# A two-layer sequence kernel: the second layer's weights split once and kept in DRAM, or split again for each block

## The chip, the cores and the metric

The kernel runs on one core of a Trainium2 chip. The core has five engines that run side by side, each through its own list of instructions in order: TensorE (PE in the rows; PEld is its weight load), VectorE (DVE), ScalarE (ACT), GpSimd (POOL) and SyncE (SP), which here issues nearly all DMA transfers. They wait for each other through semaphores. The metric is the time of one execution in microseconds on the device, the median of three runs. A second source is one profiled execution, in which the start and the length of every instruction are recorded.

## What is computed

A trunk of two layers over a sequence of 2048 positions with 1024 channels, all in float32. The part of the reference that matters here:

```python
c_act = jax.nn.silu(c)
for i in range(DEPTH):                      # DEPTH = 2
    shift, scale, gate = jnp.split(c_act @ ada_w[i] + ada_b[i], 3, axis=-1)
    h = rms_norm(x, norm_pre[i]) * (1.0 + scale[:, None, :]) + shift[:, None, :]
    if i % 2 == 0:
        p = h @ ev_w_in[j]                  # 1024 x 4224
        ...                                 # a recurrence (RWKV-7) and a gated short convolution
        y = jnp.concatenate([y_a, y_b], axis=-1) @ ev_w_out[j]
    else:
        p = h @ od_w_in[j]                  # 1024 x 3080
        ...                                 # a 31-tap convolution with LayerNorm (C), a chunked state-space scan (D)
        y = jnp.concatenate([y_c, y_d], axis=-1) @ od_w_out[j]
    x = x + gate[:, None, :] * rms_norm(y, norm_post[i])
```

The input projection `h @ od_w_in` of the second layer is the place of the change.

## The kernel before

Products run in the float32r type. To keep float32 accuracy, each operand is split into two float32r parts: `hi` is a rounded copy (made by ScalarE, `CAST w<-x`), `lo` is what is left, `raw - hi` (made by GpSimd, `TENSOR_TENSOR w<-x,w`). Three products (hi hi, hi lo, lo hi) stand for one. A weight tile is 128 output channels wide: 1024 x 128 numbers, 512 KB as it lies in DRAM (tile `x`, 128 x 1024), 1 MB when split (two tiles `w` of 128 x 2 x 512). One job is one weight tile times one block of 512 positions: 8 contraction steps with three products each, 24 products of 128 x 512 into one PSUM bank `pp`.

Layer 0 goes over two halves of the sequence with 33 weight tiles each; each tile serves two blocks. Between its products stand the steps of the recurrence (tiles `ch`, `yp`, `UV`, `S`, `SC`, `X`, `BK`). Then comes its output projection, `out_proj`. Layer 1 goes over four blocks of 512 positions; for each block all 25 weight tiles are fetched and split again, so 100 jobs. Its side work is the 31-tap convolution (`conv31`: tile `co`, 24 taps a channel group on VectorE, five on ScalarE and GpSimd through `pr` and `cs`), the scan (`ssd_chunk`: `rep`, `xd`, `xw`, `sy`, `S`), the LayerNorm (`conf_out`) and the modulated rows of the next block (`hblock`: `h`, `act`). The last output projection ends the kernel.

The class `Feed` hands out weight tiles: `fetch` loads a raw tile into `x` (ring of two), `prepare` splits it into two `w` tiles (ring `wp` of four, so two jobs). In `run_jobs`, at the start of job n, the tile of job n+1 is split and that of job n+2 fetched. The transfers of the weights, of `rep`, of the rows `h` and of the results `y` all stand in SP's one list.

Work that is not a product is written as generators in queues (`bg`, `quick`, `ev`, `aux`, `post`, `tail`, `urgent`, `slow`). A product loop calls `tick` after every second product (layer 0) or every fourth (layer 1); a tick lets the first generator of each queue take a step. In layer 0 a step is held back until a small model of the engines' load (`Clock`) allows it. `slow` holds the modulation of both layers (loads of `ada_w` into `h`) and the gate row; it is emptied before `out_proj`. The framework then puts the instructions of each engine into their final order, which can move an instruction ahead of others that were written before it.

Of the kernel before, what the change touches and what calls it, by code (L numbers as in the profile page):

```python
# [9 lines left out]
F32 = mybir.dt.float32  # L10
# [8 lines left out]
P = 128  # L19
# [51 lines left out]
class Clock:  # L71
    """Estimate of when each engine gets through what has been issued to it, by which work is spread over the products."""
# [49 lines left out]
class Feed:  # L122
    """Weight tiles of a list of jobs: fetched two jobs ahead, split one job ahead."""
# [5 lines left out]
    def fetch(self):  # L129
        if self.jobs and len(self.raw) < 2:  # L130
            self.raw.append((self.jobs[0], self.trunk.raw(self.jobs.pop(0).src)))

    def prepare(self):
        if self.raw and len(self.w) < 2:
            job, r = self.raw.pop(0)
            self.w[job] = (job.split or self.trunk.split_w)(r)


class Trunk:
    def __init__(self, ctx, tc, I, out, T, dbg=None):  # L140
# [12 lines left out]
        self.wp = pool("wp", 4)  # L153
# [62 lines left out]
    def take(self, name, shape, bufs=1, busy=None):  # L216
        """A tile of a ring, once the last steps on the one that it follows are issued; free() ends its use."""
        ring = self.rings.setdefault((id(self.t) if name != "tr" else 0, name), [])
        while len(ring) >= bufs and id(ring[-bufs]) in self.inuse:
            yield busy  # L220
        t = self.tr.tile(shape, F32, name=name) if name == "tr" else self.t.tile(shape, F32, name=name, bufs=bufs)
        ring.append(t)
        self.inuse.add(id(t))
        return t
# [24 lines left out]
    def setup(self):  # L249
# [43 lines left out]
        self.y = [[self.dram.tile([P, KT, BL], F32, name=f"y{l}_{b}") for b in range(NBLK)] for l in range(2)]  # L293
        self.x1 = [self.dram.tile([P, D], F32, name=f"x1_{t}") for t in range(self.T // P)]

# [48 lines left out]
    def split_w(self, r, pool=None, bufs=4):  # L344
        w = []
        for z in range(2):
            t = (pool or self.wp).tile([P, 2, BL], F32R, name="w", bufs=bufs)
            self.split(t[:, 0], t[:, 1], r[:, z * BL:(z + 1) * BL])
            w.append(t)
        return lambda i, k: w[k // 4][:, i, (k % 4) * P:(k % 4 + 1) * P]  # L350

# [100 lines left out]
    def hblock(self, l, blocks, spread=1, places=None):  # L452
        """Modulated rows of blocks, in halves; those of the next half are fetched and normalized ahead where there is a place for them."""
# [57 lines left out]
    def first_blocks(self, begun):  # L511
        """Blocks 0 and 1 of layer 0, and the first projections, whose products follow each part of the modulated rows."""
# [79 lines left out]
        for d in range(KT):  # L592
            while raws and raws[0][0] < d:
# [3 lines left out]
                         (lambda w: [w[:, 0], w[:, 1]])(self.wp.tile([P, 2, BL], F32R, name="w")) for _ in range(2)]  # L597
# [576 lines left out]
    def odd(self, b):  # L1174
        W = lambda ti: self.I["w_in1"][ti]
        st = {"B": [None] * 2, "C": [None] * 2, "sz": [None] * 4, "co": [None] * 4, "cg": [None] * 4}
        jobs = [Job(W(24), lambda bl, ps: self.evac_dt(b, st, ps), mm=self.mm_dt, split=self.split_dt)]
# [150 lines left out]
    def split_dt(self, r):  # L1328
        nc = self.nc
        w = self.wp.tile([P, 2, BL], F32R, name="w")  # L1330
# [174 lines left out]
def tile_trunk(ctx, tc, I, out, T):  # L1505
# [4 lines left out]
    with ExitStack() as e:  # L1510
# [6 lines left out]
        k.slow += [k.modulation(0, range(16, 24), 1), k.modulation(1, range(24), 1), k.gate_row(0)]  # L1517
        halves = lambda name: tuple(k.t.tile([P, BL], F32, name=name, bufs=2) for _ in range(2))
# [83 lines left out]
```

## Time and profile before

| what | value |
|---|---|
| median of 3 runs | 2700.67 us (2700.13 to 2702.35) |
| profiled execution, first to last instruction | 2697.7 us |
| TensorE busy | 2418.6 us, 90% |
| VectorE busy | 1867.9 us, 69% |
| GpSimd busy | 1169.7 us, 43% |
| ScalarE busy | 1018.5 us, 38% |
| moved by DMA | 218.31 MB |

Busy time is the time in which an engine has an instruction running. It says nothing of what it waits for: a VectorE instruction that is slowed by something else counts as busy for all of its length. The profiled execution divides into layer 0's projections and recurrence (to about 1480 us), its output projection (to about 1600 us), layer 1's blocks (to about 2580 us) and the last output projection. The shares differ by stage, so they are read by stage below.

### The profile page before, as it was taken

How to read it: one execution, taken by the hardware profiler on the slowest of the kernel's cores; microseconds unless marked ns; L12 is line 12 of the kernel's file. 1: busy time of each engine (PE TensorE's matmuls, PEld its weight loads, DVE VectorE, ACT ScalarE, POOL GpSimd, SP SyncE). 2: the span in 40 equal slices, each digit the busy share in tenths (PEclk: the TensorE clock that was granted, in tenths of full speed). 3: DMA queues.
4: the chain of work that ended last, by engine and by line, in shares of the span. 5: the costliest groups of instructions: out<-in, count | busy, mean ns of one | idle time of the engine just before them, and what ended most of it. 6: DMA issues, size and time to landing. Idle time of an engine off the chain costs nothing.

```text
span 2697.7 us, 35944 instructions
## 1 busy us (share of the span) xinstructions
PE 2418.6 (90%) x13408; PEld 1828.1 (68%) x13408; DVE 1867.9 (69%) x3223; ACT 1018.5 (38%) x2058; POOL 1169.7 (43%) x1274
## 2 busy tenths in 40 slices
PE   5998999999999999999999989877888788688898
PEld 3675666766757667676776877765766676576687
DVE  5897664945768466584653126699899989999821
ACT  5423322233452332323332246434644544344231
POOL 5423223232242232423224544556566556656654
PEclk9998988989899998999999999898998899798999
DMA  6352110101211011010132433222322232222343
GB/s 237 101 174 73 44 32 29 40 29 48 71 37 40 32 37 36 32 47 24 44 107 86 154 139 118 98 71 75 105 87 67 102 102 86 86 98 67 110 147 126
DMA packets 101570, 218.31 MB, mean 81 GB/s; under 512 B 7442, under 2 KB 49682, under 8 KB 101396
## 3 DMA queue, kind: packets, MB, share of 16 engines
q1 hardware_dynamic: 101252, 215.76, 23.7%
q8 instruction: 105, 1.72, 0.3%
q14 instruction: 69, 0.57, 0.1%
q10 hardware_dynamic: 144, 0.26, 0.0%
HBM read 182.37 MB, written 33.62 MB: 80 GB/s over the span
## 4 chain that ended last, share of the span: by engine, by line
PE 45%; DVE 41%; POOL 4%; issue 4%; ACT 4%; DMA 2%; SPq 0%; DVEq 0%; POOLq 0%; ACTq 0%
PE pp L111 30%; DVE co L111 12%; PE tr L111 6%; PE yp L111 5%; PE ch L111 4%; DVE pr L111 3%; DVE X L111 3%; DVE BK L111 3%; DVE rep L111 2%; DVE sx L111 1%; POOL ss L111 1%; DVE act L111 1%; DVE sy L111 1%; DVE SC L111 1%; DVE sc L111 1%
## 5 line engine op out<-in xcount | busy, mean ns | idle before, releaser
L111 PE MATMUL pp<-act,w 128*128 128x512 f32 x7000 | 1878.4, 416 | 29.1 <-DVE yo L111 13.7
L111 PEld LDWEIGHTS pp<-act,w 128*128 128x128 f32 x7000 | 1325.0, 197 | 332.5 <-DVE yo L111 15.2
L111 POOL TENSOR_TENSOR w<-x,w 128x512 fp32r<-128x512 f32 x386 | 560.7, 1458 | 548.5 <-ACT w L111 544.6
L111 DVE SCALAR_TENSOR_TENSOR co<-u,cfw,co 128x512 f32<-128x512 f32 x384 | 388.7, 1028 | 4.8 <-ACT co L111 3.5
L111 ACT CAST w<-x 128x512 fp32r<-128x512 f32 x390 | 238.6, 619 | 234.3 <-PE pp L111 181.4
L111 POOL TENSOR_SCALAR sp<-S,PL 128x64 f32<-128x64 f32 x128 | 70.4, 552 | 278.0 <-DVE S L111 273.8
L111 ACT ACTIVATE UV<-ch,scal 64x64 f32<-64x64 f32 x256 | 79.3, 310 | 246.2 <-PE ch L111 242.5
L111 POOL TENSOR_TENSOR cs<-pr,cs 128x512 f32<-128x512 f32 x80 | 126.7, 1584 | 27.1 <-ACT cs L111 17.1
L111 DVE SCALAR_TENSOR_TENSOR S<-ch,PL,sp 128x64 f32<-128x64 f32 x128 | 36.0, 282 | 146.6 <-PE ch L111 141.6
L111 ACT ACTIVATE tA<-pp 128x512 f32<-128x512 f32 x96 | 57.2, 596 | 212.5 <-PE pp L111 140.3
L111 DVE TENSOR_TENSOR ss<-ss 128x1 f32<-128x1 f32 x60 | 12.6, 211 | 167.6 <-ACT tA L111 167.5
L111 DVE COPY z<-ch 128x64 f32<-128x64 f32 x128 | 28.6, 223 | 129.2 <-PE ch L111 126.4
L111 DVE TENSOR_TENSOR pr<-X,BK 128x2 f32<-128x2 f32 (+30 forms) x248 | 112.1, 452 | 6.5
L111 POOL COPY carry<-q 128x1 f32<-128x1 f32 (+1 forms) x84 | 21.5, 256 | 195.2 <-ACT q L111 119.3
L111 DVE TENSOR_TENSOR act<-yo,act 128x256 fp32r<-128x256 f32 (+1 forms) x104 | 52.7, 531 | 64.3 <-ACT act L111 63.7
L111 POOL COPY q<-carry 128x1 f32<-128x1 f32 (+1 forms) x84 | 29.9, 356 | 143.6 <-DVE tG L111 70.1
L111 DVE TENSOR_REDUCE X<-pr 128x1 f32<-128x2 f32 (+30 forms) x248 | 86.6, 349 | 6.6
L111 POOL TENSOR_SCALAR ss<-ss 128x1 f32<-128x1 f32 x80 | 30.6, 383 | 134.1 <-DVE ss L111 105.4
L111 PE MATMUL yp<-UV,SC 128*64 128x64 f32 x512 | 84.1, 250 | 0.0
L111 POOL TENSOR_TENSOR x<-x,yo 128x512 f32<-128x512 f32 x62 | 81.2, 1330 | 5.5 <-DVE yo L111 5.5
L111 PE MATMUL yp<-S,AR 64*64 64x64 f32 x512 | 78.0, 248 | 0.0
L111 ACT ACTIVATE pr<-u,cfw 128x512 f32<-128x512 f32 x80 | 56.2, 718 | 40.3 <-POOL cs L111 40.3
(288 smaller groups left out, 3385.5 us busy)
## 6 DMA issues: line engine op xcount, KB each, us to landing
x<-in_w_in_dram SPq DMA_DIRECT2D x163, 512.0 KB, 3.5
h<-in_ada_w_dram SPq DMA_DIRECT2D x32, 512.0 KB, 3.5
x<-y SPq DMA_DIRECT2D x32, 512.0 KB, 4.2
x<-x SPq DMA_DIRECT2D x32, 512.0 KB, 3.2
y<-yo SPq DMA_DIRECT2D x32, 256.0 KB, 2.2
h<-in_w_out_dram SPq DMA_DIRECT2D x16, 512.0 KB, 4.1
x<-in_x_dram SPq DMA_DIRECT2D x16, 512.0 KB, 3.5
rep<-acs SPq DMA_DIRECT2D x16, 512.0 KB, 4.8
```

The source lines that it names most:

```text
L111: return f(*args, **kw)
```

## The change

Layer 1's 24 full weight tiles are split once, during layer 0, by a new generator `presplit` at the end of the queue `slow`. For each half tile it loads 256 KB into `psr`, splits it into `psw` (one buffer each), and stores the 512 KB of `psw` to a DRAM tile `w1_j_z`. In layer 1, `Feed.fetch` calls `parts`, which loads the two stored parts into two `w` tiles; `prepare` only hands them on. The ring `wp` has six tiles in place of four, so three jobs. The 25th tile (the one for dt, `split_dt`) and the tiles of the output projections are split as before. The scratch memory for software DMA is set to 1024 bytes. Some comments and doc strings are removed; they do nothing.

```diff
     def fetch(self):
         if self.jobs and len(self.raw) < 2:
-            self.raw.append((self.jobs[0], self.trunk.raw(self.jobs.pop(0).src)))
+            job = self.jobs.pop(0)
+            self.raw.append((job, self.trunk.parts(job.src) if isinstance(job.src, list) else self.trunk.raw(job.src)))
     def prepare(self):
         if self.raw and len(self.w) < 2:
             job, r = self.raw.pop(0)
-            self.w[job] = (job.split or self.trunk.split_w)(r)
+            self.w[job] = r if isinstance(job.src, list) else (job.split or self.trunk.split_w)(r)
...
-        self.wp = pool("wp", 4)
+        self.wp = pool("wp", 6)
...
+        self.w1 = [[self.dram.tile([P, 2, BL], F32, name=f"w1_{j}_{z}") for z in range(2)] for j in range(24)]
...
+    def parts(self, src):
+        w = []
+        for z in range(2):
+            t = self.w_tile()
+            self.nc.sync.dma_start(out=t.bitcast(F32), in_=src[z])
+            w.append(t)
+        return self.picked(w)
+
+    def presplit(self, tiles):
+        for src, parts in tiles:
+            for z in range(2):
+                r = self.st.tile([P, BL], F32, name="psr", bufs=1)
+                self.nc.sync.dma_start(out=r.rearrange("p (k t) -> p k t", k=4) if len(src.shape) == 3 else r,
+                                       in_=src[:, z * BL:(z + 1) * BL])
+                yield True
+                yield
+                w = self.st.tile([P, 2, BL], F32R, name="psw", bufs=1)
+                self.split(w[:, 0], w[:, 1], r)
+                yield
+                self.nc.sync.dma_start(out=parts[z], in_=w.bitcast(F32))
+                yield
...
-        W = lambda ti: self.I["w_in1"][ti]
+        W = lambda ti: self.w1[ti]
-        jobs = [Job(W(24), lambda bl, ps: self.evac_dt(b, st, ps), mm=self.mm_dt, split=self.split_dt)]
+        jobs = [Job(self.I["w_in1"][24], lambda bl, ps: self.evac_dt(b, st, ps), mm=self.mm_dt, split=self.split_dt)]
...
         k.slow += [k.modulation(0, range(16, 24), 1), k.modulation(1, range(24), 1), k.gate_row(0)]
+        k.slow.append(k.presplit([(I["w_in1"][j], k.w1[j]) for j in range(24)]))
...
-    nc = bacc.Bacc("TRN2", target_bir_lowering=False, num_devices=1)
+    nc = bacc.Bacc("TRN2", target_bir_lowering=False, num_devices=1, dynamic_dma_scratch_size=1024)
```

Three places show what this does to the order. First SP's list early in layer 0, behind the second load of `w2a2`; before it reads:

```order
L111 DMA w2a_1584<-in_w2a_dram 128x128
L111 DMA x<-in_w_in_dram 128x1024
L111 DMA h<-in_ada_w_dram 128x1024 x3
L111 DMA x<-in_w_in_dram 128x1024
L111 DMA h<-in_ada_w_dram 128x1024 x4
L111 DMA x<-in_w_in_dram 128x1024
```

and now, with `w_0_0_117` the DRAM tile of weight tile 0, half 0:

```order
L111 DMA w2a_1632<-in_w2a_dram 128x128
L111 DMA psr<-in_w_in_dram 128x512
L111 DMA x<-in_w_in_dram 128x1024
L111 DMA w_0_0_117<-psw 128x1024
L111 DMA psr<-in_w_in_dram 128x512
L111 DMA x<-in_w_in_dram 128x1024
L111 DMA h<-in_ada_w_dram 128x1024 x2
L111 DMA w_0_1_118<-psw 128x1024
L111 DMA h<-in_ada_w_dram 128x1024
L111 DMA x<-in_w_in_dram 128x1024
```

The loads and stores of the half tiles stand between the weight loads of layer 0 and the loads for the modulation; 48 pairs follow each other like this, the last store ahead of the fifth `y<-sc` store.

Second, GpSimd's list in layer 1, where the third block's scan steps (`ss`) and convolution (`cs`, `ccf`) alternate; before:

```order
L111 TENSOR_TENSOR w<-x,w 128x512 x3
L111 COPY ccf<-u 128x30
L111 TENSOR_TENSOR cs<-pr,cs 128x512 x3
L111 TENSOR_TENSOR w<-x,w 128x512
L111 TENSOR_TENSOR cs<-pr,cs 128x512
L111 TENSOR_TENSOR w<-x,w 128x512
L111 TENSOR_TENSOR cs<-pr,cs 128x512
L111 TENSOR_TENSOR w<-x,w 128x512
L111 TENSOR_SCALAR ss<-ss 128x1
L111 TENSOR_TENSOR ss<-ss,nhalf 128x1
```

and now:

```order
L111 TENSOR_TENSOR ss<-ss,nhalf 128x1
L111 COPY ccf<-u 128x30
L111 TENSOR_TENSOR cs<-pr,cs 128x512 x5
L111 TENSOR_SCALAR ss<-ss 128x1
L111 TENSOR_TENSOR ss<-ss,nhalf 128x1
L111 COPY ccf<-u 128x30
L111 COPY u<-ccf 128x30
L111 TENSOR_TENSOR cs<-pr,cs 128x512 x5
```

The subtractions of the weight split are gone from between the other steps; nothing takes their place.

Third, SP's list at the start of layer 1's third block, around the loads of `rep`; before:

```order
L111 DMA x<-in_w_in_dram 128x1024 x6
L111 DMA acs_15587<-at 32x128
L111 DMA rep<-acs_15587 128x1024 x2
L111 DMA x<-in_w_in_dram 128x1024 x2
L111 DMA h<-x_10_127 128x1024
L111 DMA h<-x_11_128 128x1024
L111 DMA x<-in_w_in_dram 128x1024 x2
```

and now, with `w_12_0_141` the stored part of tile 12, half 0:

```order
L111 DMA w<-w_23_1_164 128x1024
L111 DMA acs_15813<-at 32x128
L111 DMA w<-w_12_0_141 128x1024
L111 DMA rep<-acs_15813 128x1024 x2
L111 DMA w<-w_12_1_142 128x1024
L111 DMA w<-w_13_0_143 128x1024
L111 DMA w<-w_13_1_144 128x1024
L111 DMA w<-w_14_0_145 128x1024
L111 DMA w<-w_14_1_146 128x1024
L111 DMA h<-x_10_175 128x1024
L111 DMA h<-x_11_176 128x1024
```

Two loads `w` stand where one load `x` stood. Each now waits for TensorE to have read the tiles that are six back in the ring; before, a load waited for GpSimd's split of the tile two back. The order of TensorE's products in layer 1 is the same but for a few that change places.

## Rows read from the trace of the kernel before

**Rows 1.** Busy time of each engine in stretches; columns in the first line.
```profile
core 0: us, PE busy (x) PEld busy (x) DVE busy (x) ACT busy (x) POOL busy (x), PEclk, DMA share, GB/s
60.00:500.00 440.00, 407.34 (x2493) 293.39 (x2492) 311.15 (x641) 143.12 (x285) 144.99 (x187) 0.91 0.22 72
...
1600.00:1761.20 161.20, 139.45 (x659) 113.94 (x658) 106.25 (x183) 94.77 (x199) 81.88 (x86) 0.94 0.33 110
1761.20:1985.50 224.30, 180.50 (x826) 146.52 (x825) 209.80 (x296) 110.50 (x213) 130.29 (x116) 0.89 0.26 87
1985.50:2210.40 224.90, 181.21 (x829) 147.92 (x828) 209.19 (x297) 110.30 (x213) 131.04 (x116) 0.89 0.26 87
2210.40:2429.10 218.70, 176.07 (x799) 143.00 (x799) 209.95 (x280) 93.30 (x165) 128.56 (x107) 0.90 0.26 89
2429.10:2582.40 153.30, 126.69 (x555) 101.42 (x554) 127.73 (x155) 48.43 (x92) 91.01 (x76) 0.92 0.28 93
2582.40:2697.70 115.30, 107.00 (x472) 88.24 (x471) 22.42 (x40) 25.86 (x61) 56.47 (x60) 0.98 0.41 139
```

**Rows 2.** The chain of waits from 1985.5 to 2210.4 us, shares by line.
```profile
by line: DVE co L111 35.3%; PE pp L111 13.5%; DVE rep L111 5.7%; issue 5.3%; DVE sx L111 4.0%; PE tr L111 3.5%; DVE sy L111 3.3%; DVE dh L111 2.8%; DVE xd L111 1.8%; POOL ss L111 1.8%; DVE xw L111 1.6%; DVE act L111 1.6%; POOL w L111 1.4%; 
```

**Rows 3.** TensorE's waits, 1600 to 2582 us: total us, times, longest.
```profile
PE tr L111 <- ACT sy L111: 51.5, 12, 7.0
```

**Rows 4.** VectorE in order of time, 2004 to 2016 us: start, us, instruction.
```profile
2004.14 0.67 DVE L111 TENSOR_TENSOR sy<-sy,yp 128x512 f32<-128x512 f32 x1
...
2010.42 1.75 DVE L111 SCALAR_TENSOR_TENSOR co<-u,cfw,co 128x512 f32<-128x512 f32 x1
2012.10 1.30 DVE L111 TENSOR_SCALAR rep<-rep,acs 128x128 f32<-128x128 f32 x1
2013.33 0.74 DVE L111 SCALAR_TENSOR_TENSOR co<-u,cfw,co 128x512 f32<-128x512 f32 x1
...
2015.25 0.28 DVE L111 TENSOR_SCALAR rep<-rep,acs 128x128 f32<-128x128 f32 x1
```

**Rows 5.** GpSimd in order of time, 1998 to 2013 us.
```profile
1998.75 8.27 POOL L111 TENSOR_TENSOR cs<-pr,cs 128x512 f32<-128x512 f32 x5 [1.76 <-ACT cs L111]
...
2010.28 3.04 POOL L111 TENSOR_TENSOR w<-x,w 128x512 fp32r<-128x512 f32 x2
```

**Rows 6.** GpSimd's groups, 1985.5 to 2210.4 us: count, busy us, mean ns, idle before.
```profile
L111 POOL TENSOR_TENSOR w<-x,w 128x512 fp32r<-128x512 f32 x48 | 73.4, 1540 | 56.6 <-ACT w L111 56.6
L111 POOL TENSOR_TENSOR cs<-pr,cs 128x512 f32<-128x512 f32 x20 | 31.0, 1550 | 8.4 <-ACT cs L111 5.5 <-ACT pr L111 2.0
```

**Rows 7.** VectorE's two costliest groups, 1985.5 to 2210.4 us.
```profile
L111 DVE SCALAR_TENSOR_TENSOR co<-u,cfw,co 128x512 f32<-128x512 f32 x97 | 99.5, 1042 | 1.1 <-ACT co L111 0.9
L111 DVE TENSOR_SCALAR rep<-rep,acs 128x128 f32<-128x128 f32 x32 | 13.7, 469 | 0.0
```

**Rows 8.** The waits of SP's list, 1600 to 2600 us.
```profile
SPq L111 <- POOL w L111: 676.6, 99, 16.4
```

**Rows 9.** DMA issues: count, KB each, median us from issue to landing.
```profile
x<-in_w_in_dram SPq DMA_DIRECT2D x163, 512.0 KB, 3.5
...
x<-x SPq DMA_DIRECT2D x32, 512.0 KB, 3.2
...
X<-in_consts_dram SPq DMA_DIRECT2D x8, 256.0 KB, 3.0
```

**Rows 10.** SP in order of time, 0 to 620 us: two places in its list.
```profile
68.29 0.33 SPq L111 DMA_DIRECT2D w2a<-in_w2a_dram  x1
...
538.83 0.33 SPq L111 DMA_DIRECT2D y<-sc  x1
```

**Rows 11.** The chain of waits from 60 to 500 us, shares by line.
```profile
by line: PE pp L111 27.6%; PE tr L111 10.2%; PE ch L111 6.7%; PE yp L111 6.0%; DVE h L111 5.9%; DVE BK L111 4.9%; DVE X L111 4.7%; DVE pr L111 4.3%; DMA h<-in_ada_w_dram 3.5%; issue 3.3%; DVE SC L111 2.9%; DVE sc L111 2.3%; DVE tD L111 2.2%
```

**Rows 12.** Groups of all engines, 60 to 500 us: the weight splits.
```profile
L111 POOL TENSOR_TENSOR w<-x,w 128x512 fp32r<-128x512 f32 x40 | 56.4, 1412 | 73.5 <-ACT w L111 73.2
...
L111 ACT CAST w<-x 128x512 fp32r<-128x512 f32 x40 | 24.6, 618 | 46.6 <-PE pp L111 46.2
```

More of the change, by code (lines that the diff above doesn't have):

```diff
@@ L342, in split, with w_tile, split_w, picked @@
         (eng or self.nc.gpsimd).tensor_tensor(out=lo, in0=raw, in1=hi.bitcast(F32), op=ALU.subtract)
-    def split_w(self, r, pool=None, bufs=4):
+    def w_tile(self):
+        return self.wp.tile([P, 2, BL], F32R, name="w")
+    def split_w(self, r):
         w = []
         for z in range(2):
-            t = (pool or self.wp).tile([P, 2, BL], F32R, name="w", bufs=bufs)
+            t = self.w_tile()
             self.split(t[:, 0], t[:, 1], r[:, z * BL:(z + 1) * BL])
             w.append(t)
+        return self.picked(w)
+    def picked(self, w):
         return lambda i, k: w[k // 4][:, i, (k % 4) * P:(k % 4 + 1) * P]
+    def parts(self, src):
+        w = []
+        for z in range(2):
+            t = self.w_tile()
+            self.nc.sync.dma_start(out=t.bitcast(F32), in_=src[z])
+            w.append(t)
+        return self.picked(w)
+    def presplit(self, tiles):
[11 more added lines that the diff above has]
+                yield
     def proj_part(self, ps, w, a, k):
@@ L596, in first_blocks @@
                 parts = [[t.tile([P, BL], F32R, name=m, bufs=2) for m in names] if n == 2 else
-                         (lambda w: [w[:, 0], w[:, 1]])(self.wp.tile([P, 2, BL], F32R, name="w")) for _ in range(2)]
+                         (lambda w: [w[:, 0], w[:, 1]])(self.w_tile()) for _ in range(2)]
                 for z in range(2):
@@ L1329, in split_dt @@
         nc = self.nc
-        w = self.wp.tile([P, 2, BL], F32R, name="w")
+        w = self.w_tile()
         r3 = r.rearrange("p (k c) -> p k c", k=KT)
```

## The prediction, made before the changed kernel was run

> **What bounds the kernel now.** I read the busy times by stage first [rows 1]. In layer 0 (60 to 500 us as a sample) TensorE is busy for 407 of 440 us. Layer 1 is different. [...] Second, the chain of waits over one period [rows 2]: the eight VectorE lines named there (co, rep, sx, sy, dh, xd, xw, act) make 56.1%, products 13.5%. So layer 1 is paced by VectorE, and TensorE waits for it: over layer 1 its largest wait is 51.5 us for sy, which is a VectorE chain with a short GpSimd and ScalarE end [rows 3].
>
> Third, why VectorE is so busy. The same tap of the 31-tap convolution (co) takes 0.74 us at 2013.3 and 1.75 us at 2010.4; a rep step takes 0.28 us at 2015.2 and 1.30 us at 2012.1 [rows 4]. GpSimd, at 2010.28 to 2013.32, runs two w subtractions, the low part of a weight split [rows 5]. Both slow instructions start inside them, both quick ones outside. An addition that reads PSUM (sy with yp, 2004.14) takes 0.67 us although GpSimd is then in its five cs additions of 1998.75 to 2007.0. So a GpSimd subtraction costs VectorE about 1.0 us when VectorE just then has an instruction with its operands in SBUF: 1.75 - 0.74 = 1.01, and 1.30 - 0.28 = 1.02.
>
> [...]
>
> **Part 1: 192 splits leave layer 1.** 24 tiles of 2 halves for 4 blocks are 192 ScalarE casts and 192 GpSimd subtractions; 48 of each stay, in layer 0. In a period 48 subtractions take 73.4 us of GpSimd [rows 6]. What they cost VectorE has two ends. High: 1.0 us each, 48 us a period. Low: only what two groups show. The 97 taps have a mean of 1042 ns against 0.74 us alone, 29 us; the 32 rep steps 469 ns against 0.28 us, 6 us [rows 7]; of these 35 us the w share by GpSimd's busy time is 73.4/(73.4 + 31.0) = 0.70, so 25 us or 0.5 us each. I take 0.75 us, the middle, since the other VectorE groups (sx, sB, sC, dh) have not been counted in the low end: 36 us a period, VectorE from 209 to 173 us.
>
> How much of the 36 us shortens a period? Low: VectorE is on the chain for 56% of 224.9 = 126 us of its 209, so 0.6 x 36 = 22 us. High: all 36 and the 1.4% (3 us) that w itself has on the chain [rows 2], 39 us. Middle 31 us. Then a period is about 194 us, with VectorE busy for 173 and TensorE for at most 181 (less, if its clock rises); both are nearly full, so what is late next is TensorE. Three periods: -92 us (bounds with both prices: -42 to -135). The other 48 subtractions belong to the ramps: 1600 to 1761, where TensorE is already busy for 139 of 161 us, and 2429 to 2582, where VectorE is busy for 128 of 153 us [rows 1]. They are 36 us of VectorE; I take two thirds, -24 us (-8 to -42). The last output projection (from 2582, TensorE 107 of 115 us) has none of these splits: 0. ScalarE's casts are off the chain: 0 by themselves.
>
> **Part 2: the parts are fetched, 1 MB a tile instead of 0.5.** The order of SP shows two loads w where one x stood. Before, a fetch waited for GpSimd's split of an earlier tile (676.6 us of SP waiting between 1600 and 2600 us) [rows 8]; now it waits for TensorE to be through with the job three back, as the ring holds three jobs. Between that and its own first product lie two jobs of 24 products, 48 x 0.227 (107.00 us for 472) = 10.9 us at the least. Two loads of 512 KB land in 3.5 us each, 7 us if one came after the other [rows 9]. So the fetch is hidden by the two jobs' products: 0. If that cover were gone, a job would wait for some 4 us, 16 us a period. The traffic of a period rises by 24 x 0.5 MB = 12 MB on 87 GB/s x 225 us = 20 MB, so to about 0.42 of the DMA engines' time from 0.26 [rows 1]. Queued behind a waiting fetch on SP are rep loads, h loads and y stores; they stood behind fetches before, so I put 0 on them.
>
> **Part 3: the 48 half tiles that layer 0 now splits.** Each is a load of 256 KB (psr), a cast, a subtraction and a store of 512 KB (psw), with one buffer each. In the order of SP the first psr load stands behind the second w2a2 load, at 68.3 us in the trace of before, and the last psw store ahead of the fifth y store from sc, at 538.8 us [rows 10]: 48 halves in 470 us, 9.8 us each. VectorE: 48 x 0.75 = 36 us, where it is busy for 311 of 440 us and holds 27% of the chain (the seven lines h, BK, X, pr, SC, sc, tD) [rows 11]: 10 us on the path (0 to 36). ScalarE: the next cast waits for the last store. Cast 0.62, subtraction 1.41 [rows 12] and the landing of 512 KB, 3.2 us [rows 9], are 5.2 us, with issues of 0.33 us on SP 5.7 us; the load (3.0 us) runs beside the store. That fits into 9.8 us on the mean, but in the first 150 us h loads that wait for VectorE stand between, and what is queued behind a waiting cast on ScalarE are the copies that TensorE waits for. I take 8 us (0 to 60). SP's x loads for layer 0 stand behind psw stores that wait for GpSimd; the ring of six gives them a job more of lead, which hides it: 0. Together +18 us.
>
> **Sum.** -92 - 24 + 18 = -98 us on the profiled execution of 2697.7 us: 2599.7. The median of the runs, 2700.67, lies 3.0 us above that, so 2602.7, said as 2603 us.
>
> **The rivals.** (a) Slower: the single psr and psw buffers make ScalarE wait, in its order, for a DMA at each of the 48 halves, and behind it the UV copies of the recurrence, on which TensorE waits. The place is 68 to 539 us. One landing of 3.2 us reaching TensorE each time costs 154 us: 2700.7 - 116 + 10 + 154 = 2749 us. It decides from (116 - 10)/48 = 2.2 us a half on. For it: one buffer, and SP in order. Against it: 9.8 us of spacing against 5.7, and the products of later tiles that stand between the recurrence's steps on TensorE. (b) The gain is there but small: TensorE's waits stay, because sy still passes GpSimd, ScalarE and two turns of TensorE, and weights come late behind y stores that wait for VectorE. With the low price and the low share 14 us a period, 8 for the ramps and 18 lost: about 2670 us. For it: TensorE is busy for 80% already. (c) The gain is larger: VectorE's price is 1.0 us and both engines run full. 45 us a period, 40 for the ramps, layer 0 free: 2700.7 - 175 = 2526 us. For it: the slow rows; against it: two engines with 160 and 180 us of work each that wait for each other in turn. (d) No change, because something else paces layer 1: nothing on the chain says so; 2701 us.
>
> **How the numbers follow.** Forecast 0.66; (a) 0.07, (b) 0.13, (c) 0.11, (d) 0.03. The forecast's own bounds are 2560 to 2650; the range of 2540 to 2675 takes in (b) and the edge of (c) and leaves (a), (d) and most of (c) out. Faster by over 0.2% (about what a measurement can tell here) is the forecast with (b) and (c), 0.90; within 0.2% is (d), 0.03; slower is (a), 0.07.
>
> **What would show it.** In the profile after: the group of w subtractions down by 192 with 48 psw ones in its place; the mean of the co taps at about 0.8 us instead of 1.04; VectorE's busy time in a layer 1 period near 173 us and the period near 194; SP waiting for TensorE at w loads, and TensorE with hardly a wait for them; the end of the first layer's products within 20 us of 1480. Wrong would be the prediction if co stays at 1.0 us (the cs additions would then be the whole cause), if TensorE waits for w loads, or if the layer 0 stretch to 540 us grows by more than 60 us with ScalarE waiting for psr loads or psw stores.

## The result, and the profile after

The changed kernel takes 2665.93 us (2659.73 to 2674.55), 0.9886 of the time before (interval 0.9857 to 0.9915), or 34.5 us less. The forecast was 2603 us, 98 less. The sign and the range held, the size did not: about a third of the gain came. Two executions are left out of the times below, each at a lower granted clock and longer than the others of its kernel (the presplit alone, 2758.41 us at 0.911 against 2710.90 to 2744.67 at 0.915 to 0.931; the one with both engines subtracting, 2763.47 us at 0.905 against 2712.78 to 2728.38 at 0.922 to 0.926), and since they are the profiled ones, of these two kernels only times are used.

The profiled execution after takes 2672.8 us against 2697.7 of before, 24.9 less; it was the longest of the four. Four marks in SP's list, found by the same loads in both, show where it went: the first load of `w_out` at the end of layer 0's recurrence (one pair of `w_out` loads stands earlier, at 750 us before, and is not meant), the first load of `rep` in layer 1's first and fourth block, and the end. A mark is read from one execution. The kernel that only passes the presplit's steps, below, takes the time of the one before and has its first mark at 1364 us instead of 1375, so differences of some 10 us at this mark are not read as an effect.

| stretch | before, us | after, us | difference |
|---|---|---|---|
| start to the first `w_out` load of the group at layer 0's end | 1374.8 | 1421.8 | +47.1 |
| to the first `rep` load (output projection 0, first jobs of layer 1) | 280.5 | 303.9 | +23.4 |
| to the fourth block's first `rep` load (three periods) | 676.4 | 566.2 | -110.2 |
| to the end (rest of block 4, output projection 1) | 366.1 | 380.9 | +14.8 |

**Layer 1 did what it should, and more.** The three periods after, which answer to the rows from 1761.2 to 2429.1 us of [rows 1] (columns as there):

```profile
1725.70:1917.70 192.00, 175.75 (x843) 144.91 (x842) 159.78 (x275) 83.10 (x162) 57.02 (x60) 0.97 0.52 170
1917.70:2105.50 187.80, 174.40 (x833) 143.46 (x832) 170.28 (x296) 85.60 (x164) 64.36 (x68) 0.95 0.53 171
2105.50:2291.90 186.40, 174.01 (x837) 143.47 (x836) 172.22 (x292) 81.88 (x150) 60.26 (x64) 0.96 0.56 186
```

A period is 186 to 192 us long, VectorE is busy for 160 to 172 of it instead of 209, GpSimd for 57 to 64 instead of 130, and TensorE's granted clock is 0.95 to 0.97 instead of 0.89 to 0.90. The groups of VectorE in the second of these periods answer to [rows 7], and the second fence, all 128 rep steps (count, shortest/median/longest ns, first and last start) of before and then of after, to [rows 4]:

```profile
L111 DVE SCALAR_TENSOR_TENSOR co<-u,cfw,co 128x512 f32<-128x512 f32 x96 | 76.6, 814 | 2.1 <-ACT co L111 1.9
L111 DVE TENSOR_SCALAR rep<-rep,acs 128x128 f32<-128x128 f32 x32 | 7.8, 284 | 0.1
```

```profile
L111 DVE TENSOR_SCALAR rep<-rep,acs x128: 268/276/1414, 1662.1 to 2467.2; 128x128 f32<-128x128 f32 x128
```

```profile
L111 DVE TENSOR_SCALAR rep<-rep,acs x128: 273/283/292, 1730.8 to 2409.2; 128x128 f32<-128x128 f32 x128
```

No rep step is longer than 0.292 us any more; 1.41 us was the longest. TensorE's and SP's waits between 1650 and 2540 us, against [rows 3] and [rows 8]:

```profile
PE tr L111 <- ACT sy L111: 16.6, 8, 5.1
```

```profile
SPq L111 <- PE pp L111: 457.5, 176, 10.7
SPq L111 <- POOL w L111: 56.3, 9, 15.4
```

The fetch of the parts waits for TensorE, and no wait of TensorE for a `w` load is among its largest, although the DMA engines' share rose from 0.26 to 0.52 to 0.56.

Of the slow rows that the forecast started from, the trace shows more than was read. Of the 384 taps (co) before, the 175 that overlap no addition or subtraction on GpSimd take 0.73 to 0.75 us, and the 109 that overlap w subtractions and no other of them 1.27 us on the mean (counted from the trace). After, 58 taps that overlap cs additions alone still take 1.22 us on the mean: most of what is left of the price is that of the convolution's own additions.

**The output projections got slower**, for which the forecast had no term. SP in order of time in output projection 0, before and after (start, us, instruction):

```profile
1522.59 0.53 SPq L111 DMA_DIRECT2D x<-y  x1
1525.08 0.32 SPq L111 DMA_DIRECT2D x<-x  x1
1528.06 0.33 SPq L111 DMA_DIRECT2D x<-in_x_dram  x1
1533.48 0.52 SPq L111 DMA_DIRECT2D x<-y  x1
```

```profile
1551.15 0.33 SPq L111 DMA_DIRECT2D x<-in_x_dram  x1
1553.65 0.32 SPq L111 DMA_DIRECT2D x<-x  x1
1556.30 0.52 SPq L111 DMA_DIRECT2D x<-y  x1
1564.88 0.33 SPq L111 DMA_DIRECT2D x<-in_x_dram  x1
1567.38 0.32 SPq L111 DMA_DIRECT2D x<-x  x1
1569.98 0.53 SPq L111 DMA_DIRECT2D x<-y  x1
```

A tile of 128 positions takes 10.9 us before (1522.59 to 1533.48) and 13.7 after (1556.30 to 1569.98). Before, the load of the next y rows (`x<-y`) goes out 2.5 us ahead of the store of the residual rows (`x<-x`); after, 2.6 us behind it, as long as a store takes to land here (2.6 us in the median of the ten between 1500 and 1640 us). The chain of waits between 1530 and 1640 us after says so:

```profile
by line: PE pp L111 52.8%; DMA x<-x 9.9%; DMA x<-y 7.9%; POOL x L111 6.8%; DVE ss L111 5.0%; POOL w L111 4.6%; POOL ss L111 4.2%; issue 3.7%; DVE yo L111 3.5%; ACT tA L111 2.3%; POOLq L111 0.2%; ACTq L111 0.1%; ACT w L111 0.1%
```

The y rows and the residual rows come from one ring `x` of two buffers. The reading is that before, the y rows always take the one and the residual rows the other, and that after, they trade places at each tile, so that a load of y rows must wait until the residual rows in its buffer have been stored. No row names a buffer; the first run below tests it.

**Layer 0 got slower by 47 us.** The stretch to the first `w_out` load, before and after:

```profile
0.00:1374.80 1374.80, 1288.98 (x8085) 921.29 (x8086) 928.51 (x1873) 467.46 (x962) 449.92 (x602) 0.93 0.18 60
```

```profile
0.00:1421.80 1421.80, 1322.69 (x8084) 940.38 (x8085) 956.39 (x1873) 495.56 (x1012) 520.34 (x652) 0.90 0.25 85
```

TensorE makes the same products and is busy for 33.7 us more, at a mean granted clock of 0.90 instead of 0.93, and idle for 13.4 us more (99.1 against 85.8). VectorE runs the same 1873 instructions in 27.9 us more. The 48 subtractions are this group, and GpSimd's wait for the casts is 89 us:

```profile
L111 POOL TENSOR_TENSOR psw<-psr,psw 128x512 fp32r<-128x512 f32 x48 | 67.2, 1399 | 92.5 <-ACT psw L111 89.2
```

### The profile page after: what moved, and what is told of

Same layout as the page of the kernel before. It is cut to its first block, busy times and chain, and to the rows that moved or that the text cites. A ratio compares the mean times of both kernels' runs of the same rounds, so it can differ in the third digit from the quotient of the medians.

```text
span 2672.8 us, 35838 instructions
## 1 busy us (share of the span) xinstructions
PE 2440.7 (91%) x13408; PEld 1837.3 (69%) x13408; DVE 1759.1 (66%) x3223; ACT 945.1 (35%) x1914; POOL 964.2 (36%) x1130
## 4 chain that ended last, share of the span: by engine, by line
PE 47%; DVE 34%; POOL 7%; issue 4%; DMA 4%; ACT 4%; SPq 0%; POOLq 0%; DVEq 0%; ACTq 0%
PE pp L111 32%; DVE co L111 7%; PE tr L111 6%; PE yp L111 5%; PE ch L111 5%; DVE pr L111 4%; DVE X L111 3%; DVE BK L111 3%; POOL ss L111 2%; DMA x<-y 1%; DVE rep L111 1%; DVE SC L111 1%; DVE yo L111 1%; DVE sc L111 1%; DVE act L111 1%
## 5 line engine op out<-in xcount | busy, mean ns | idle before, releaser
L111 POOL TENSOR_TENSOR w<-x,w 128x512 fp32r<-128x512 f32 x194 | 268.7, 1388 | 359.1 <-ACT w L111 355.2
L111 DVE SCALAR_TENSOR_TENSOR co<-u,cfw,co 128x512 f32<-128x512 f32 x384 | 322.1, 855 | 7.7 <-ACT co L111 6.6
L111 ACT CAST w<-x 128x512 fp32r<-128x512 f32 (+1 forms) x198 | 122.5, 625 | 272.4 <-DMA x<-y 186.5
L111 DVE TENSOR_TENSOR ss<-ss 128x1 f32<-128x1 f32 x60 | 21.6, 361 | 213.9 <-ACT tA L111 213.5
L111 POOL TENSOR_TENSOR cs<-pr,cs 128x512 f32<-128x512 f32 x80 | 127.4, 1593 | 28.9 <-ACT cs L111 14.8
L111 POOL TENSOR_TENSOR psw<-psr,psw 128x512 fp32r<-128x512 f32 x48 | 67.2, 1399 | 92.5 <-ACT psw L111 89.2
```

The source lines that it names most:

```text
L111: return f(*args, **kw)
```

## The experiments

All times are medians of three executions or more, and each ratio (with its 95% interval) is to executions of the kernel before that were taken beside them.

**Where the output projections lost: two fixed slots.** The changed kernel, with the ring of two taken apart into two tags of one buffer each.

```diff
...                                                             # other users take the two tags in turn
-    raws[t] = self.raw(self.y[l][b][:, :, o:o + P])
+    raws[t] = self.raw(self.y[l][b][:, :, o:o + P], "xb" if t == 1 else "xa")
...
-    x = self.x_rows(l, t, self.xp.tile([P, D], F32, name="x"))
+    x = self.x_rows(l, t, self.xp.tile([P, D], F32, name="xb", bufs=1))
```

> The changed kernel, but the two raw buffers have fixed uses in the output projections: one for the y rows (xa), one for the residual rows (xb), as they came to lie in the kernel before. Theory 1 (the ring of six made the two buffers trade places, so that each y load waits for the store of the residual rows): the step from tile to tile in both output projections goes from 13.7 back to 10.9 us, about 13 steps each, so some 60 to 70 us less than the changed kernel's 2666: 2600 us (2590 to 2615). Rival (the output projections are slow because of the clock or because of DMA traffic): the step stays at 13.7 us and the time at 2660 to 2670 us. Layer 1's periods stay at 187 us by both.

Measured: 2613.93 us, 0.969 (0.9661 to 0.9718), 52 us below the change. SP's list again, with `xa` for the y rows:

```profile
1553.26 0.53 SPq L111 DMA_DIRECT2D xa<-y  x1
1555.75 0.32 SPq L111 DMA_DIRECT2D x<-xb  x1
1558.71 0.33 SPq L111 DMA_DIRECT2D xb<-in_x_dram  x1
1564.14 0.53 SPq L111 DMA_DIRECT2D xa<-y  x1
```

The tile is back at 10.9 us, with the y load ahead of the store. By the four marks this kernel stands to the one before at +42, +1, -109 and -18 us: the second and fourth stretch are where the trade of slots had cost its 52 us (22 and 33 us by these marks), and 42 us of layer 0 are left.

**Which part of the change trades the slots, and which costs layer 0: each part alone.** The ring of six without the presplit, and the presplit without the rest (ring of four, layer 1 splits as before, nobody reads the stored parts).

```diff
-        self.wp = pool("wp", 4)
+        self.wp = pool("wp", 6)                 # the ring alone
...
-        W = lambda ti: self.w1[ti]
+        W = lambda ti: self.I["w_in1"][ti]      # the presplit alone, wp of 4
```

> The kernel before with nothing changed but the ring of split weight tiles, six in place of four (and the smaller scratch memory that makes room). Theory 1 (the deeper ring alone makes the raw buffers trade places): both output projections step at 13.7 us, 60 to 70 us more than before, 2765 us; layer 1's periods stay at 225 us. Rival: the ring is harmless, 2695 to 2705 us. For layer 0: if the 47 us that the changed kernel lost there came from the ring, the first load of the output weights comes at 1420 us here too; if from the half tiles split there, at 1375 us.

> The kernel before (ring of four, layer 1 splits its weights for each block) with the 48 half tiles split and stored in layer 0 beside it; nobody reads the stored parts. Theory 2 (layer 0's loss is the price of these 48 splits): layer 0 ends some 35 to 47 us later, 2735 to 2747 us. Rival (the loss came from the ring or from the clock): 2700 to 2710 us. Both output projections step at 10.9 us.

Measured: the ring alone 2757.61 us, 1.022 (1.0187 to 1.0253). Its first `w_out` load comes at 1367 us, no later than before, and its output projection steps by 13.6 us (1487.11, 1500.72, 1514.29). So the ring of six trades the slots by itself and costs layer 0 nothing. This kernel has the smaller scratch memory too, but so have the kernels below with a ring of four, and there the last tile of the projection takes 10.9 us as before (1571.1 to 1582.0 in the one without GpSimd). The presplit alone takes 2728.10 us (2710.90 to 2744.67), 1.0113 (1.0047 to 1.0178): layer 1 and both rings are as before, so the loss is put down to the presplit in layer 0, by the time alone and with a wide spread.

**Is it the single buffers?** The same with two buffers for `psr` and for `psw`.

```diff
-                r = self.st.tile([P, BL], F32, name="psr", bufs=1)
+                r = self.st.tile([P, BL], F32, name="psr", bufs=2)      # psw too
```

> As e3, with two buffers each for psr and psw in place of one. Theory 2a (the price in layer 0 is ScalarE waiting, in its order, for the loads of psr and the stores of psw; 55 us of such waits were seen): most of it goes, at most 15 us over before, 2700 to 2715 us. Theory 2b (the price is the GpSimd subtractions that hold VectorE up): the same as e3, 2735 to 2747 us.

Measured: 2765.08 us, 1.0252 (1.0219 to 1.0285), slower still, with the first `w_out` load at 1433 us. The halves only follow each other faster (the last `psr` load at 449.5 us instead of 561.9 in the changed kernel). ScalarE's wait for the `psr` loads fell to 32 us, from 60 in the changed kernel, and the time rose. Neither theory had that, and rival (a) of the prediction, a wait for the single buffers, is not what costs the time.

**What of the presplit costs: take away one part at a time.** From the presplit alone: GpSimd's subtraction replaced by a second cast; transfers only; no instruction at all.

```diff
-                self.split(w[:, 0], w[:, 1], r)
+                for i in range(2):
+                    self.nc.scalar.copy(out=w[:, i], in_=r)      # no GpSimd
```

> As the run with the presplit alone (layer 1 splits as before and does not read the stored parts), but GpSimd's subtraction of the presplit is replaced by a second ScalarE cast, so that 48 loads, 48 stores and 96 ScalarE casts remain and no GpSimd work; the low part that is stored is wrong and unread. That run took 2711 to 2745 us against 2700.6, and its first w_out load, the end of layer 0's recurrences, came at 1427 against 1375 us. Theory A, the price is GpSimd's subtraction holding VectorE: 2695 to 2710, first w_out load at 1370 to 1390. Theory B, ScalarE's waits for the landing of the fetched halves (67 us in 19 waits there): 2725 to 2750, as with the subtraction or a little more for the 48 casts of 0.62 us added. Theory C, the transfers, and theory D, the order of the other instructions: 2725 to 2745, first w_out load at 1415 to 1430.

```diff
+        w = self.st.tile([P, 2, BL], F32R, name="psw", bufs=1)          # ahead of the loop, set to zero once
...
-                self.split(w[:, 0], w[:, 1], r)                         # transfers only
```

> The presplit's 48 loads of 256 KB and 48 stores of 512 KB stay, its casts and subtractions are left out (the stores write a tile of zeros, which nobody reads; layer 1 splits as before). Theory C, the transfers and SP's queue are the price: 2725 to 2745, first w_out load at 1415 to 1430. Theories A (GpSimd holding VectorE) and B (ScalarE waiting for landings): 2695 to 2710, first w_out load at 1370 to 1390. Theory D, the shifted order: 2725 to 2745 here, and the same in the run that only passes the steps.

```diff
             for z in range(2):
-                ...                                                     # every instruction of the presplit
                 yield True
                 yield
                 yield
                 yield
```

> The presplit passes its 192 steps of the slow queue and issues nothing (layer 1 splits as before), so only the order in which the rest of layer 0 is issued shifts. Theory D, the shifted order alone costs layer 0 its 45 us: 2725 to 2745, first w_out load at 1415 to 1430. Theories A, B and C: 2695 to 2705, first w_out load at 1370 to 1380.

Measured: without GpSimd 2708.42 us, 1.0029 (1.0007 to 1.0051), first `w_out` load at 1380; transfers only 2692.77, 0.9971 (0.9945 to 0.9996), at 1365; steps only 2702.47, 1.0003 (0.9985 to 1.002), at 1364. Theories B, C and D fall: 48 loads, 48 stores, 96 casts and ScalarE's waits for `psr` (56 us of them) cost 6 us together. By the marks the loss is there only with GpSimd's subtraction; by the times alone the step from the presplit alone (1.0113, 1.0047 to 1.0178) to this kernel without GpSimd is just clear of noise, and the runs in which VectorE subtracts, below, make it firm.

**Elsewhere: the presplit in output projection 0**, where VectorE, ScalarE and GpSimd have room, on the fixed slots.

```diff
+        k.slow.append(k.presplit([(I["w_in1"][j], k.w1[j]) for j in used]))   # behind k.drain(k.slow)
...
+                with self.tc.issue_after(after):        # behind the third y load
                     self.nc.sync.dma_start(out=r..., in_=src[:, z * BL:(z + 1) * BL])
```

> The run with fixed slots for the y rows and the residual rows (2613.93 us, first w_out load at 1417), with the presplit moved out of layer 0: its loads are issued behind the third y load of output projection 0, tiles in the order in which layer 1 uses them, so its 48 halves lie in the 250 us in which VectorE and ScalarE are busy 76 to 78 us and GpSimd 106. If the price in layer 0 comes of the presplit's place there, whichever of A to D it is: first w_out load back at 1370 to 1385, output projection 0 still near 11 us a tile, 2565 to 2585 us. Rival: the 48 subtractions of 1.4 us (67 us) stand in GpSimd's queue ahead of the projection's own splits and the 48 stores ahead of its y loads in SP's: three halves a tile, up to 4.2 us on each of 16 tiles, 2614 - 42 + 67 = about 2640.

Measured: 2658.7 us, 0.9852 (0.9817 to 0.9886), 45 us worse than with the presplit in layer 0, beyond the rival too. Layer 0 had its time back (first `w_out` load at 1376), but a tile of the projection took 13.0 us, and TensorE then stood still. TensorE's and VectorE's longest waits between 1400 and 1750 us:

```profile
PE tr L111 <- ACT tA L111: 58.9, 1, 58.9
```

```profile
DVE cfw L111 <- DMA w<-psw: 77.1, 1, 77.1
```

With one buffer each, a half takes some 6 us from one subtraction to the next (1717.47 to 1723.70), and the 48 did not fit into the stage: layer 1's set-up (`cfw`) waited for the last store from `psw`, a tile of layer 0's pool.

**Is it GpSimd's wait in its queue, or its subtraction?** On the fixed slots, each of the presplit's instructions is pinned (an edge that fixes the order and waits for nothing) behind the instruction last issued to its engine, and the steps are spread over layer 0 (the subtractions lie from 329 to 1495 us, five of them behind the first `w_out` load); then the same with VectorE subtracting.

```diff
...                                                       # load and store in the same way, behind("D")
-                self.split(w[:, 0], w[:, 1], r)
+                with behind("A"):
+                    self.nc.scalar.copy(out=w[:, 0], in_=r)
+                for _ in range(3):
+                    yield
+                with behind("G"):                        # or behind("V") and nc.vector
+                    self.nc.gpsimd.tensor_tensor(out=w[:, 1], in0=r, in1=w[:, 0].bitcast(F32), op=ALU.subtract)
```

> The run with fixed slots (2613.93 us, first w_out load at 1417), with each load, cast, subtraction and store of the presplit pinned behind the instruction that was last issued to its engine when its step came, and 11 steps a half instead of 4: the halves lie over all of layer 0 (204 to about 1430 us), and GpSimd no longer reaches a subtraction before the ScalarE cast that it waits for is due. The run without the subtraction gave layer 0 nearly all of its time back, so the price is GpSimd's, in one of two ways. Theory A1, GpSimd's 48 subtractions hold VectorE and the engine's own later work for as long as they run: they still run, so 2605 to 2617 and the first w_out load at 1405 to 1420. Theory A2, GpSimd stood waiting for the cast (92 us by 572 us in the run with the presplit alone), with the recurrences' sp, carry and BK behind it in its queue: that wait goes, so 2570 to 2590 and the first w_out load at 1375 to 1390.

> As the pinned and spread presplit on the fixed slots, but VectorE makes the 48 subtractions, at about 0.6 us each: 29 us of an engine that is busy 880 of 1375 us in layer 0. Theory A1 (GpSimd's subtraction held VectorE for about 0.75 us each, so that VectorE pays either way): 2600 to 2615, first w_out load at 1400 to 1415. Theory A2 (GpSimd's queue was the price): 2575 to 2592, first w_out load at 1375 to 1390.

Measured: with GpSimd 2625.83 us, 0.9738 (0.9706 to 0.9771); with VectorE **2563.78 us**, 0.9511 (0.9471 to 0.9552), the best of all kernels here. The stretch to the first `w_out` load, GpSimd and then VectorE:

```profile
0.00:1419.20 1419.20, 1318.04 (x8075) 937.45 (x8076) 943.60 (x1873) 490.94 (x1008) 515.91 (x647) 0.90 0.24 82
```

```profile
0.00:1355.30 1355.30, 1262.95 (x8084) 904.58 (x8085) 953.53 (x1916) 489.94 (x1008) 466.44 (x604) 0.95 0.26 86
```

With GpSimd, most of the waits did go against the fixed slots (ScalarE's for `psr` from 59.5 to 1.4 us, GpSimd's for the casts from 86 to 31), and layer 0 was no shorter for it (1419 against 1417 us): theory A2 falls. With VectorE subtracting, the engine runs 43 instructions more and is busy for 10 us more, and yet layer 0 is 64 us shorter, nearly all of it TensorE's busy time (55 us) at a clock of 0.95 instead of 0.90. Theory A1 in its plain form, that VectorE pays either way, missed this kernel by 36 us, and theory A2 missed it too, by 11 us in time and 20 at the mark. VectorE's own subtractions are short, 0.77 us each where about 0.6 was expected:

```profile
L111 DVE TENSOR_TENSOR psw<-psr,psw 128x512 fp32r<-128x512 f32 x48 | 36.8, 766 | 4.5 <-ACT psw L111 4.4
```

**Does the engine alone do it?** The fixed slots with VectorE subtracting, nothing pinned or spread: one argument more in the call, `self.split(w[:, 0], w[:, 1], r, self.nc.vector)`.

> The run with fixed slots (2613.93 us, first w_out load at 1417) with one change: VectorE makes the presplit's subtractions; nothing is pinned or spread. The engine alone is the gain: 2562 to 2582, first w_out load at 1355 to 1380. Pinning and spreading are needed too, since VectorE then stands waiting for the cast as GpSimd did (92 us by 572 us with the presplit alone): 2600 to 2640, first w_out load at 1400 to 1440.

Measured: 2576.77 us (2570.71 to 2595.41), 0.9562 (0.9517 to 0.9607), first `w_out` load at 1372. The engine alone is 37 of the 50 us between the fixed slots and the best kernel; the other 13 are hardly more than the spread of these executions.

**Does a GpSimd subtraction cost as much when nobody waits for it?** First, 48 subtractions of a tile of zeros from itself, added to the kernel without GpSimd's subtraction (`none` for both operands); then 48 of two resident tiles, added to the presplit alone with VectorE subtracting, pinned and spread; last that kernel without them.

```diff
+                with behind("G"):
+                    self.nc.gpsimd.tensor_tensor(out=out, in0=one, in1=two, op=ALU.subtract)
```

> The run in which the presplit's subtraction was replaced by a second ScalarE cast (2708 us against 2703, first w_out load at 1380), with 48 subtractions given back to GpSimd that wait for nothing: a tile of zeros from itself into a tile that nobody reads, each behind the instruction last issued to GpSimd at that step (the stored low part is wrong and unread, layer 1 splits as before). [...] Theory A1 (they hold VectorE and GpSimd's queue for 1.4 us each): 2725 to 2745, first w_out load at 1410 to 1427. Theory A2 (the wait for the cast was the price): 2705 to 2715, first w_out load at 1380 to 1390.

> The presplit alone (layer 1 splits as before and does not read the stored parts), pinned and spread, with VectorE making the real subtractions; GpSimd makes 48 more at the same places, of two resident tiles into a third that nobody reads, so that it waits for nothing and nothing waits for it. With VectorE's subtractions alone the first w_out load came at 1355, with GpSimd's real ones, pinned alike, at 1419; 2703 is the time before. Theory A1, GpSimd's subtraction of two operands beside VectorE is the price as such: first w_out load at 1400 to 1420, 2725 to 2750. Theory A3, it is GpSimd's place in the chain of load, cast, subtraction and store: first w_out load at 1355 to 1380, 2685 to 2712.

> The run in which both engines subtracted, with GpSimd's 48 extra subtractions taken out and nothing else changed (the presplit pinned and spread, VectorE subtracting, layer 1 splitting as before and not reading the stored parts). With them it took 2724 us. Theory A1, GpSimd's subtractions as such are the price of layer 0: 2675 to 2695, first w_out load at 1350 to 1370. Theory A3, they cost only a little when nobody waits for them and the place in the chain was the price: 2708 to 2722, first w_out load at 1390 to 1415.

Measured: the tile from itself 2721.29 us, 1.0088 (1.0059 to 1.0118), 13 us above its kernel without them (2708.42, 1.0029). That lies between the ranges of theories A2 and A1. Its first `w_out` load, at 1383 us, is in A2's range, but stands earlier in the order (7998 of TensorE's products ahead of it, 8084 without the subtractions); the last y load of output projection 0 came at 1592 us with them and at 1582 without, though all 48 lie before 1107 us. These 48 took 1.04 us each in the median, not the 1.4 of the real ones (1.399 on the mean in the changed kernel). Two tiles 2723.68 us, 1.0075 (1.0053 to 1.0098); without them 2710.73, 1.0048 (1.0021 to 1.0076), first `w_out` load at 1375. By the medians that is 13 us again, by the ratios 7 us with an interval that takes in 0. Theory A3 had the time of the last kernel (2708 to 2722), but not its mark; the time with the two tiles lies between the ranges of A3 and A1.

So 48 subtractions that nobody waits for cost about 13 us, 0.27 us each, shown by the first pair and not firmly by the second. Real ones, in the chain of load, cast, subtraction and store, cost 37 us more than VectorE's (2613.93 - 2576.77) or, pinned, 62 (2625.83 - 2563.78). The two figures do not stand on one base: these kernels have the ring of six and the stored parts in use, those with idle subtractions the ring of four. On the ring of four the real ones cost 20 us (2728.10 - 2708.42, the first of them with a spread of 34 us) or, with two buffers, 57 (2765.08 - 2708.42). That real ones are dearer than idle ones is therefore not shown.

## Why the prediction was wrong, step by step

- **Layer 1's periods: right.** Forecast 194 us a period and VectorE at 173; measured 186 to 192 and 160 to 172. The three periods gave 110 us, forecast 92, inside its bounds. The mean of the co taps came out at 814 ns where about 0.8 us was expected, and the w subtractions went from 386 to 194, the 192 that were named. What was short is the price: VectorE's busy time fell by 127 us in the three periods, 0.88 us for each of 144 subtractions instead of 0.75. Of the 127 us, 110 left the time, a share of 0.87, about the 31 of 36 us that was taken. TensorE's clock in the periods, 0.96 instead of 0.89, was named in passing ("less, if its clock rises") and not priced. A rep step took 1.41 us at most with the subtractions and 0.29 without; what makes a VectorE instruction longer beside a subtraction is not shown. Layer 1's periods and ramps together gave 11 us more than forecast (110 + 17 against 92 + 24).
- **The ramps: inside their bounds.** Forecast -24 (-8 to -42); with fixed slots the second and fourth stretch are at +1 and -18.
- **The fetch: right.** SP waits for TensorE, TensorE hardly for `w`. The DMA engines' share came out at 0.52 to 0.56 and not at 0.42: the 32 MB were spread over the old period of 225 us and not over the shorter one.
- **"The last output projection ... has none of these splits: 0": the first failure.** Neither output projection has a term for the ring of two raw buffers that it shares with the weight loads; the last one is put at 0 because nothing is split there, the first is not named. The ring of six appears only as a gain, a job more of lead. Changing its depth reordered the users of the other ring, and the price was 52 us: 2.7 us on each of some 20 tiles (in the first half of projection 0 the tiles wait for the y rows anyway). It could have been seen in the order of SP's list after the change (y load ahead of the store before, behind it now); the prediction reads that order in layer 0 and in layer 1, not between them.
- **Part 3, "+18 us": the second failure, by size.** Forecast 10 us through VectorE and 8 through ScalarE; measured 47. VectorE's own price was about right (48 x 0.75 = 36 forecast, 27.9 measured), but "10 us on the path" was not: TensorE is busy for 94% of layer 0, and the 10 us are VectorE's share of the chain, with no term for TensorE's clock. TensorE lost 13 us in waits and 34 in products at a lower granted clock (0.90 instead of 0.93). ScalarE's 8 us were not there (6 us at the most, in the kernel without GpSimd). Of the marks for a wrong prediction, the stretch to 540 us grew by 34 us, below the 60 named; a further 13 came after the last half, where no presplit instruction is left, about as much as this mark differs between executions. The end of the first layer's products, forecast within 20 us of 1480, was not read by itself; the first mark moved by 47.
- **Sum.** -98 with +52 for the slots and +29 for layer 0 is -17; the periods gave 18 more than forecast, the ramps 7 less, which makes -28; the profiled execution shows -25. Rival (b), a small gain of 2670 us, named nearly the time, but by other causes than those that ruled: it kept layer 1's gain small, and layer 1 gave more than forecast. That the range took in 2666 us, through (b), was luck.
- **The kernel that keeps the gain.** Fixed slots and VectorE's subtractions: -19 in layer 0, +8, -106 and -19 us by the four marks, -137 in all. Where the 19 us in layer 0 come from was not separated: with the ring of four the same pinned presplit has its mark at 1375 us, that of before.

## What to carry to other kernels

When a ring's depth changes, look at who shares the other rings too: two users of two buffers may trade places without any line of code on them having changed (52 us here), and one load that stands behind a store shows it in the order of the list. When work is moved to a stage that another engine paces, do not price it by its own engine's share of that stage's chain alone (10 us forecast here; the stretch grew by 47); ask also what the pacing engine's clock becomes (0.90 here instead of 0.93). And when a step moves, ask anew which engine should do it: what had gone to GpSimd, to spare VectorE in layer 1 (busy for 209 of 225 us), belonged on VectorE in layer 0 (busy for 928.51 of 1374.8 us before), where it brought the first `w_out` load from 1419 to 1355 us.

## What the runs showed of the hardware that was not expected

**The granted clock stood at half for 20 us while TensorE was busy.** TensorE's rows at a step of the recurrence (columns as in [rows 1]), before and then after:

```profile
210.00:220.00 10.00, 3.17 (x35) 2.91 (x36) 9.76 (x20) 1.18 (x3) 2.44 (x3) 0.60 0.37 119
220.00:230.00 10.00, 10.00 (x79) 7.79 (x79) 9.91 (x12) 2.40 (x4) 4.15 (x3) 0.72 0.23 79
230.00:240.00 10.00, 10.00 (x74) 6.21 (x70) 2.21 (x5) 5.43 (x10) 1.43 (x3) 0.66 0.24 79
240.00:250.00 10.00, 9.82 (x79) 6.33 (x79) 8.13 (x17) 6.03 (x14) 7.94 (x9) 1.00 0.00 0
```

```profile
210.00:220.00 10.00, 3.66 (x15) 2.55 (x14) 10.00 (x23) 0.78 (x2) 2.06 (x3) 0.93 0.86 303
220.00:230.00 10.00, 3.83 (x36) 3.02 (x36) 9.00 (x16) 2.29 (x4) 3.08 (x4) 0.50 0.61 191
230.00:240.00 10.00, 10.00 (x87) 8.19 (x86) 9.91 (x13) 3.02 (x5) 4.52 (x4) 0.72 0.39 124
240.00:250.00 10.00, 10.00 (x61) 5.63 (x58) 3.42 (x7) 5.33 (x10) 2.10 (x4) 0.62 0.36 145
250.00:260.00 10.00, 10.00 (x55) 6.33 (x54) 4.72 (x9) 1.14 (x3) 7.10 (x7) 0.50 0.31 100
260.00:270.00 10.00, 10.00 (x43) 5.68 (x43) 3.84 (x13) 5.32 (x12) 0.80 (x2) 0.51 0.00 0
```

In both TensorE waits (3.17 and 3.66 us busy of ten), and its granted clock is low in the same ten us (0.60) or in the next (0.50). Before, it is back at full speed (1.00) from 240 us on; after, the wait goes on into the next ten us (3.83 us busy), the clock is higher from 230 to 250 (0.72, 0.62), and from 250 to 270 it stands at half (0.50, 0.51) although TensorE is busy all the time. That the wait brings the clock down is not shown: in the kernel before it stands at 0.51 from 396 to 427 us with TensorE busy all the time (31.00 of 31 us), as it was in the ten us ahead (10.00 us, at 1.00). In layer 0 as a whole TensorE's products at full clock would take about the same (1288.98 x 0.93 and 1322.69 x 0.90 are 1199 and 1190 us); by this estimate the difference of 47 us is in the clock and in 13 us of waits.

**With GpSimd's subtraction layer 0 grew by more than VectorE's busy time.** In four kernels with it as a part of the presplit in layer 0 (the changed one, fixed slots, two buffers, pinned) the first `w_out` load came at 1417 to 1433 us; in nine without it, that of before among them, at 1355 to 1380 (and at 1383, earlier in the order, with the tile from itself). VectorE's busy time to that load is only 15 us (pinned) to 28 us (the changed kernel) above that of before, while the load came 44 and 47 us later.

**Still open** is how a subtraction that goes with some 0.3 to 0.6 us more of VectorE's busy time (15 and 28 us for 48) goes with a lower TensorE clock in layer 0 (0.90 in the pinned and the changed kernel, 0.93 before, 0.95 with VectorE subtracting). Whether the path is VectorE's longer instructions or GpSimd's own later steps, which stand behind the subtraction in its list, was not separated, nor whether a real subtraction costs more than one that nobody waits for. The kernels differ in the order of their other instructions as well.
